# A hybrid encoder step on one core: queues filled in the order of the kernel's own estimate, with measured durations

## The chip, the cores and the metric

The kernel runs on one core of a Trainium2 chip. The metric is the device time of one execution in microseconds (us). Engines: TensorE (PE) multiplies matrices, VectorE (DVE), ScalarE (ACT) and GpSimd (POOL) work on elements, SyncE (SP) issues most transfers. Each engine runs its own queue of instructions in the order in which the program was written out; an instruction waits for semaphores of the others.

## The reference

One inference step of a two-layer encoder for 512 prompt tokens and 32 sample tokens, model width 1024, all in float32:

```python
def run_trunk(x, pos, mem_k, mem_v, states, ln_g, ln_b, ffn_up, ffn_down, xa_q, xa_o, mixer_params):
    for layer in range(DEPTH):
        x = post_norm(x, 0.5 * swiglu(x, ffn_up[layer, 0], ffn_down[layer, 0]), ln_g[layer, 0], ln_b[layer, 0])
        if layer % 2 == 0:
            y, st = mixer_ab(x, pos, *states[layer], *mixer_params[layer])
        else:
            y, st = mixer_c(x, *states[layer], *mixer_params[layer])
        x = post_norm(x, y, ln_g[layer, 1], ln_b[layer, 1])
        x = post_norm(x, cross_attn(x, mem_k[layer], mem_v[layer], xa_q[layer], xa_o[layer]), ...)
        x = post_norm(x, 0.5 * swiglu(x, ffn_up[layer, 1], ffn_down[layer, 1]), ln_g[layer, 3], ln_b[layer, 3])
```

`post_norm` is a layer norm of `ALPHA * x + sub`, `swiglu` has 2816 inner features, `cross_attn` 4 heads over 256 memory rows. `mixer_ab` is a gated linear recurrence (RG-LRU) beside a chunkwise retention. `mixer_c` is RWKV-7: projections and low-rank gates, and then for each token and each of 16 heads of 64

```python
def step(S, inp):
    r_t, w_t, k_t, v_t, kk_t, b_t = inp
    sa = jnp.einsum('bhvk,bhk->bhv', S, -kk_t)
    S = S * w_t[:, :, None, :] + sa[..., None] * b_t[:, :, None, :] + v_t[..., None] * k_t[:, :, None, :]
    return S, jnp.einsum('bhvk,bhk->bhv', S, r_t)
```

Outputs are the trunk's results for both token sets, the memory's keys and values of both layers, and all the states.

## The kernel before

**Tiling.** Tokens are columns, features are partitions. Half A holds 256 prompt tokens, half B the other 256 and the 32 sample tokens (288 columns). Weights come in granules of 128 output features and 1024 input features. ScalarE writes a granule's rounded copy, VectorE or GpSimd the remainder (`_split`), and a linear layer takes 24 PE products per granule and half: three products of the parts times eight blocks of the input. Stages in order: ffn00, mix0, xa0, ffn10 for layer 0, ffn01, mix1, xa1, ffn11 for layer 1. The halves run staggered, so that the products of one half stand under the norms, the attention and the recurrences of the other. PSUM tiles are named mm (linear layers and the recurrence's preparation) and ax (the rest); names in the listings end in numbers that only tell buffers apart. XA, XHA and XLA are half A's values and their split parts, XB and so on half B's; within the recurrence these names stand for the space that it takes over.

**What sets the order.** Each piece of work is a Python generator, a task. Its operations go through methods such as `mm`, `tt`, `gtt`, `act`: each calls `plan` with an engine and a duration. `Clock.op` puts the operation into the first gap on the engine's line of time after its operands are ready, and the start it finds becomes the instruction's priority; tasks of a negative band see a line on which only they stand. The task that is earliest by this clock runs next. `ett` asks the clock which of VectorE and GpSimd would be through first and takes that engine, so a duration can also choose an engine. After everything is emitted, the tile framework fills each engine's queue: line 2082 asks it to do so by a simulation of its own (`schedule_with_timeline_sim=True`), which takes the priorities as a ranking among what it finds ready.

**The recurrence.** It runs in chunks of 32 tokens, in blocks of 64: four blocks of A, four of B, and one of the 32 sample tokens; nine blocks, 17 chunks. Per block, `wkv_prep` (line 1797) works out keys and decays, starting with a GpSimd multiplication (arena from HLA or HLB and pv, 128x512), and makes 16 products per quarter (64x64) that give a triangular matrix; it is stored to scratch memory (dn). `wkv_solve` (line 1873) loads it (P from dn), inverts it by 31 pairs of dependent GpSimd steps on P and LC, stores the result (dz from LC) and loads it as transposed blocks (W from dz). `wkv_load` transposes keys and values, `wkv_chain` (line 1947) carries the state through the chunks, its first product on the solved block being ax from arena and W (128x64); `wkv_norm` does the head norm. Half B's low-rank gates are 128x288 products of XB and HHB with HLB and VB.

Of the kernel before, what the change touches and what calls it, by code (L numbers as in the profile page):

```python
# [102 lines left out]
class Res:  # L103
    """Things that are taken and given back, with the times from which they are free."""
# [27 lines left out]
class Line:  # L132
    """The spans of time in which an engine is taken; a later comer may fill a gap."""
# [28 lines left out]
class Clock:  # L162
    """An estimate of when instructions run, in ns: what an engine does and what its operands wait for.
    It orders the emission and the engines' queues, and nothing else rests on it."""
# [24 lines left out]
    def ready(self, outs, ins=()):  # L189
        """When the operands of a transfer are free and written."""  # L190
        t = self.now
        for ap in ins:
            c, q, f = self.area(ap)
            t = max(t, c[0, q, f].max())
        for ap in outs:
            c, q, f = self.area(ap)
            t = max(t, c[:, q, f].max())
        return t

    def renew(self, old, new):  # L200
        """A tile takes over the room of an older one."""
# [47 lines left out]
class Arena:  # L249
# [26 lines left out]
    def top(self, n):  # L276
        """The last n elements."""
# [50 lines left out]
class Arenas:  # L328
    """Several arenas as one."""
# [44 lines left out]
class Kern(Clock):  # L374
# [13 lines left out]
    def mm(self, out, lhsT, rhs, start=True, stop=True):  # L388
        n = free_size(rhs)
        if lhsT.dtype == F32R:  # L390
            cost = (n if n >= 256 else max(4 * n, 128)) / 2.4 + 2
        else:
            cost = 4 * (max(n, 62) / 2.4) + 2
# [8 lines left out]
    def _v(self, out, ins, fast=False):  # L402
        fast = fast and all(t.space != PSUM for t in ins)
        self.plan("v", 70 + free_size(out) / (1.92 if fast else 0.96), [out], ins)
# [5 lines left out]
    def gtt(self, out, a, b, op=ALU.mult):  # L410
        self.plan("g", 150 + free_size(out) * 2.0, [out], [a, b])
        self.nc.gpsimd.tensor_tensor(out, a, b, op=op)  # L412

    def ett(self, out, a, b, op=ALU.mult, lag=0.0):
        """On the engine that is through first; GpSimd has to be ahead by some ns."""
# [5 lines left out]
        dv, dg = 70 + n / 0.96, 150 + n * 2.0  # L421
# [27 lines left out]
    def gmemset(self, out, v):  # L449
        self.plan("g", 50 + free_size(out) * 0.83, [out], [])  # L450
        self.nc.gpsimd.memset(out, v)

    def scan(self, out, a, b, ini):
        self._v(out, [a, b])
# [16 lines left out]
    def act(self, out, a, f=AF.Copy, bias=None, scale=1.0, accum=None):  # L471
        dur = (60 if a.space == PSUM else 100) + free_size(out) / 1.2
        dur += 93 * ((bias is not None and not isinstance(bias, float)) + (not isinstance(scale, float)))
# [25 lines left out]
    def sigmoid(self, out, a, bias=None, half=None):  # L499
        """1 / (1 + exp(-a - bias)) = (1 + tanh((a + bias) / 2)) / 2; half: bias / 2."""  # L500
# [66 lines left out]
    def lend(self, slots, raws):  # L567
        """Slots and buffers of the weights for another use."""
# [9 lines left out]
    def stream(self, granules, after=(), limit=None, first=0):  # L578
        """Granules that are loaded one after another, from when the streams before them are through."""
# [5 lines left out]
    def pump(self):  # L585
        """Loads of weights and their splits, as far ahead as the room allows; when the next one can go."""
# [16 lines left out]
    def _load(self, s):  # L603
        """Loads a granule, or says when it could."""
# [46 lines left out]
    def linear(self, hf, xh, xl, kc=8, m=128):  # L651
        """One granule of the main stream against a half's split columns: a PSUM bank."""
# [49 lines left out]
def load_params(K):  # L702
    """Vectors of features as columns of one tile, by way of rows of 128 and transposes."""
# [125 lines left out]
def streams(K, gran, at):  # L829
    """Granules are loaded once for both halves, but for stretches of SOLO where one half is ahead, so  # L830
    that its products fill the other one's waits: for norms, attention and the recurrences."""
# [54 lines left out]
def split(K, hi, lo, src, k=0):  # L886
    """src = hi + lo, each with the 12 bits that a float32r product takes."""
# [7 lines left out]
def load_x(K, h):  # L895
    """Rows of x by way of the room for the products, as columns and their split."""
# [52 lines left out]
def store_states(K):  # L949
    """The states that were collected as columns."""  # L950
# [51 lines left out]
def out_piece(K, h, j, ps, first=True, last=True):  # L1002
    """x <- ALPHA * x + sub, a part of sub at a time.

    With the last part go the sums for the norm: the columns are shifted by the mean c of their first half,
    so that the mean of squares less the squared mean cancels no more than a bit."""
# [46 lines left out]
def rsqrt2(K, out, v, tmp, eps=None):  # L1053
    """out = -2 / sqrt(v + eps): exp(-ln / 2) and a Newton step."""
# [67 lines left out]
def mem_kv(K):  # L1122
    """Keys and values of the memory, both layers: features first in scratch (keys), rows first out.

    It fills the others' gaps, so it keeps a weight slot, a load buffer and a PSUM bank of its own."""
# [64 lines left out]
def give_kv(K, *tags):  # L1190
    """Slots' space for the split keys of a head and for its split values."""
# [45 lines left out]
def attend(K, h, l, hd, q, hh, hl, c0, m, qe, fin):  # L1237
    """Columns c0..c0+m of a half against one head's memory: prompt's own or the sample's cache.
    The weights of the values take the queries' place."""
    nc = K.nc  # L1240
# [83 lines left out]
def setup_mix0(K):  # L1324
# [26 lines left out]
    # -8 softplus(-lam) = -8 (max(-lam, 0) + 2 atanh(u / (2 + u))), u = exp(-|lam|)  # L1351
# [148 lines left out]
def rsqrt_small(K, out, v, tmp, eps):  # L1500
    """1 / sqrt(v + eps) for few columns: a guess from the bits and three Newton steps."""
# [100 lines left out]
def lora_weights(K, h):  # L1602
    """The first factors of the low-rank gates, as they are and with the mix of tokens folded in."""
# [91 lines left out]
def wkv_norm(K, w):  # L1695
    """The heads' norm, the bonus and the gate, 64 tokens at a time."""
# [34 lines left out]
def wkv(K):  # L1731
    """RWKV-7's recurrence by chunks of 32 tokens, 64 tokens prepared at a time.
# [355 lines left out]
```

## Time and profile before

| what | us |
|---|---|
| median of three runs | 3022.41 (3020.9 to 3025.26) |
| span of the profiled execution | 3028.7 |
| PE busy | 2833.4 |
| VectorE busy | 1743.4 |
| ScalarE busy | 1276.8 |
| GpSimd busy | 830.1 |

The page divides the span into 40 slices of about 76 us. PE is at 9 tenths nearly everywhere; the slices in which it is lower lie at 500 to 800 us (layer 0's mixer and attention) and at 1860 to 2540 us (the recurrence of layer 1). The clock granted to PE, too, is below full in these places alone. PE work that runs at half clock counts as busy for twice as long, so busy time and clock are read together.

### The profile page before, as it was taken

Reading aid. Unit: us, or ns where it says so; the run is one execution under the profiler, and the core shown is the slowest. Engines: PE = TensorE matmul, PEld = TensorE weight load, DVE = VectorE, ACT = ScalarE, POOL = GpSimd, SP = SyncE. Lnnn points to the kernel's source line nnn. Section 1 sums busy time; section 2 is a strip of 40 time slices with the busy share of each in tenths; the row PEclk is TensorE's granted clock in tenths of the full one; section 3 lists DMA queues with packets and bytes.
Section 4 is the critical chain, followed back from the end, with each engine's and each line's share of the span. In section 5 each row is a group of like instructions: output and inputs, shape, how many; then the busy total and the mean of one; then the engine's idle time right before and its main releaser. Section 6 shows DMA issues by size and latency. Waiting matters only on the chain.

```text
span 3028.7 us, 54637 instructions
## 1 busy us (share of the span) xinstructions
PE 2833.4 (94%) x22456; PEld 2716.3 (90%) x22456; DVE 1743.4 (58%) x3099; ACT 1276.8 (42%) x2184; POOL 830.1 (27%) x1088
## 2 busy tenths in 40 slices
PE   9999998998999999999999898888878889999998
PEld 8999998998998999989999897776767779998997
DVE  5333337677767333365355756674675666767655
ACT  4223233665545222234244343343435455655544
POOL 2001104333313000032011212466375543422301
PEclk9999999999999999999999998788778879999999
DMA  6443443322332232322356453122223135645563
GB/s 182 126 119 115 130 119 97 88 68 81 98 98 84 85 90 84 89 87 77 90 155 179 120 168 106 39 65 62 69 73 87 49 98 174 177 141 157 169 176 93
DMA packets 626331, 330.56 MB, mean 109 GB/s; under 512 B 45480, under 2 KB 620160, under 8 KB 626080
## 3 DMA queue, kind: packets, MB, share of 16 engines
q1 hardware_dynamic: 617952, 317.06, 36.8%
q0 software_dynamic: 3488, 9.44, 1.0%
q8 instruction: 176, 2.88, 0.4%
q10 hardware_dynamic: 4640, 0.56, 0.1%
q14 instruction: 75, 0.61, 0.1%
HBM read 313.09 MB, written 13.92 MB: 108 GB/s over the span
## 4 chain that ended last, share of the span: by engine, by line
PE 66%; DVE 10%; POOL 9%; DMA 7%; ACT 5%; issue 3%; SPq 0%; ACTq 0%; DVEq 0%; POOLq 0%
PE mm L395 60%; PE ax L395 4%; POOL LC L412 3%; POOL P L412 3%; DMA P<-dn 3%; DVE W L408 2%; ACT arena L486 1%; ACT W L486 1%; DVE arena L408 1%; DMA wr<-in_ffn_up 1%; PE ax L400 1%; DVE arena L432 1%; POOL arena L412 1%; ACT L2049 1%; DVE XB L408 1%
## 5 line engine op out<-in xcount | busy, mean ns | idle before, releaser
L486 ACT ACTIVATE W<-wr 128x1024 fp32r<-128x1024 f32 (+1 forms) x558 | 577.0, 1038 | 737.4 <-PE mm L395 560.0
L408 DVE TENSOR_TENSOR W<-wr,W 128x1024 fp32r<-128x1024 f32 (+1 forms) x455 | 561.5, 1236 | 551.7 <-ACT W L486 542.8
L395 PE MATMUL mm<-XHB,W 128*128 128x288 f32 x3840 | 585.1, 302 | 14.1 <-ACT XHB L486 4.7
L395 PE MATMUL mm<-XHA,W 128*128 128x256 f32 x3840 | 538.4, 290 | 28.9 <-ACT XHA L486 11.6
L395 PEld LDWEIGHTS mm<-XHB,W 128*128 128x128 f32 x3840 | 532.4, 191 | 25.0 <-ACT XHB L486 5.8
L395 PEld LDWEIGHTS mm<-XHA,W 128*128 128x128 f32 x3840 | 499.7, 194 | 39.7 <-ACT XHA L486 16.0
L412 POOL TENSOR_TENSOR W<-wr,W 128x1024 fp32r<-128x1024 f32 (+1 forms) x103 | 251.0, 2439 | 606.2 <-ACT W L486 550.6
L395 PE MATMUL mm<-XLB,W 128*128 128x288 f32 x1984 | 318.7, 300 | 0.7 <-DVE XLB L408 0.7
L395 PE MATMUL mm<-HHB,W 128*128 128x288 f32 x1920 | 291.0, 301 | 11.4 <-ACT W L486 4.4
L395 PEld LDWEIGHTS mm<-XLB,W 128*128 128x128 f32 x1984 | 283.0, 190 | 3.2 <-DVE XLB L408 1.1
L395 PE MATMUL mm<-XLA,W 128*128 128x256 f32 x1984 | 284.7, 283 | 0.0
L395 PEld LDWEIGHTS mm<-HHB,W 128*128 128x128 f32 x1920 | 267.0, 191 | 15.0 <-ACT W L486 5.3
L395 PE MATMUL mm<-HHA,W 128*128 128x256 f32 x1920 | 265.7, 288 | 5.9 <-POOL W L412 2.2
L395 PEld LDWEIGHTS mm<-XLA,W 128*128 128x128 f32 x1984 | 259.1, 190 | 0.3 <-DVE XLA L408 0.2
L395 PEld LDWEIGHTS mm<-HHA,W 128*128 128x128 f32 x1920 | 247.1, 192 | 8.8 <-POOL W L412 2.6
L486 ACT ACTIVATE arena<-mm 128x256 f32<-128x256 f32 (+4 forms) x292 | 112.2, 387 | 305.1 <-PE mm L395 287.5
L432 DVE SCALAR_TENSOR_TENSOR arena<-mm,arena 128x288 f32<-128x288 f32 (+1 forms) x176 | 77.2, 439 | 157.7 <-PE mm L395 149.0
L395 PE MATMUL mm<-HLB,W 128*128 128x288 f32 x896 | 144.3, 301 | 0.3 <-DVE HLB L408 0.3
L412 POOL TENSOR_TENSOR P<-LC,P 128x66 f32<-128x66 f32 (+24 forms) x279 | 113.5, 407 | 84.6 <-DMA P<-dn 64.6
L395 PEld LDWEIGHTS mm<-HLB,W 128*128 128x128 f32 x896 | 130.1, 193 | 0.6 <-DVE HLB L408 0.5
L395 PE MATMUL mm<-HLA,W 128*128 128x256 f32 x896 | 129.3, 284 | 0.0
L412 POOL TENSOR_TENSOR LC<-LC,P 128x66 f32<-128x66 f32 (+24 forms) x279 | 115.0, 412 | 20.5
(426 smaller groups left out, 3612.0 us busy)
## 6 DMA issues: line engine op xcount, KB each, us to landing
wr<-in_ffn_up SPq DMA_DIRECT2D x246, 512.0 KB
wr<-in_ffn_down SPq DMA_DIRECT2D x96, 448.0 KB
wr<-in_l_w_rkv SPq DMA_DIRECT2D x48, 512.0 KB
wr<-in_ffn_down SPq DMA_DIRECT2D x40, 512.0 KB
wr<-in_l_w_in SPq DMA_DIRECT2D x24, 512.0 KB
wr<-in_l_w_out SPq DMA_DIRECT2D x24, 512.0 KB
wr<-in_xa_q SPq DMA_DIRECT2D x24, 512.0 KB
wr<-in_xa_o SPq DMA_DIRECT2D x24, 512.0 KB
```

Of the source, the lines that this page charges most:

```text
L395: self.nc.tensor.matmul(out, lhsT, rhs, start=start, stop=stop)
L400: self.nc.tensor.transpose(out, in_, self.ident[k0:k0 + k, k0:k0 + k])
L408: self.nc.vector.tensor_tensor(out, a, b, op=op)
L412: self.nc.gpsimd.tensor_tensor(out, a, b, op=op)
L432: self.nc.vector.scalar_tensor_tensor(out, a, s, b, op0=op0, op1=op1)
L486: return self.nc.scalar.activation(out, a, f, bias=bias, scale=scale, **kw)
L2049: nc.scalar.preload_act_table_set(name)
```

## The change

Two edits. The durations that the methods hand to `plan` are replaced by others: a float32r product of 256 columns and more costs n/2.4 + 13 ns instead of n/2.4 + 2, a small float32 product at least 108 ns divided by `side`, the number of products that the array takes side by side; VectorE's fixed part is 147 ns instead of 70, GpSimd's 190 + 2.1 n instead of 150 + 2 n, ScalarE's 165 or 204 instead of 60 or 100, and a scan has a cost of its own. And the framework's own simulation is switched off, so that the queues are filled by the priorities. Docstrings and comments are dropped, which moves line numbers below `mm` by one. No operation is added or removed but that a few splits of weights change engines.

```diff
-    def mm(self, out, lhsT, rhs, start=True, stop=True):
+    def mm(self, out, lhsT, rhs, start=True, stop=True, side=1):
+
         n = free_size(rhs)
         if lhsT.dtype == F32R:
-            cost = (n if n >= 256 else max(4 * n, 128)) / 2.4 + 2
+            cost = n / 2.4 + 13 if n >= 256 else max(4 * n / 2.4, 108.0) + 2
         else:
-            cost = 4 * (max(n, 62) / 2.4) + 2
+            cost = max(4 * n / 2.4, 108.0) / side + 2
...
-        self.plan("v", 70 + free_size(out) / (1.92 if fast else 0.96), [out], ins)
+        self.plan("v", 147 + free_size(out) / (1.92 if fast else 0.96), [out], ins)
...
-        self.plan("g", 150 + free_size(out) * 2.0, [out], [a, b])
+        self.plan("g", 190 + free_size(out) * 2.1, [out], [a, b])
...
-        dv, dg = 70 + n / 0.96, 150 + n * 2.0
+        dv, dg = 147 + n / 0.96, 190 + n * 2.1
...
-        self.plan("g", 50 + free_size(out) * 0.83, [out], [])
+        self.plan("g", 95 + free_size(out) * 0.86, [out], [])
...
-        self._v(out, [a, b])
+        self.plan("v", 195 + free_size(out) * 2.0, [out], [a, b])
...
-        dur = (60 if a.space == PSUM else 100) + free_size(out) / 1.2
-        dur += 93 * ((bias is not None and not isinstance(bias, float)) + (not isinstance(scale, float)))
+        dur = (165 if a.space == PSUM else 204) + free_size(out) / 1.2
+        dur += 88 * ((bias is not None and not isinstance(bias, float)) + (not isinstance(scale, float)))
...
-            K.mm(pr[32 * q:32 * q + 32, g * 64:g * 64 + 64], X[0:96, hd, 32:64], Y[0:96, hd])
+            K.mm(pr[32 * q:32 * q + 32, g * 64:g * 64 + 64], X[0:96, hd, 32:64], Y[0:96, hd], side=4)
...
-    with tile.TileContext(nc, schedule_with_timeline_sim=True) as tc:
+    with tile.TileContext(nc, schedule_with_timeline_sim=False) as tc:
```

How the order moves, at two places. The first is PE's queue at the first solve: from the last key products of block 0 (XLA, 64x64) to the first product on the solved block (ax from arena and W, 128x64). Before, some rows of the stretch, its end whole:

```order
L395 MATMUL mm_64<-XLA_17671 64x64 x8
L395 MATMUL mm_66<-XLA_17671 64x64 x8
...
L395 MATMUL ax_70<-XB_98,HLB_17823 128x288
L395 MATMUL ax_70<-HHB_17886,HLB_17823 128x288
L400 MATMUL ax_67<-identt,VA_16458 32x128 x4
...
L395 MATMUL mm_65<-XHB_99,W_3_73 128x288 x8
L395 MATMUL mm_65<-XLB_100,W_3_73 128x288 x8
...
L395 MATMUL mm_63<-XLB_100,W_4_74 128x288 x8
L395 MATMUL mm_65<-XHB_99,W_3_73 128x288
L395 MATMUL ax_68<-arena_79,W_114_17676 128x64 x4
L395 MATMUL mm_64<-W_111_17673 64x64 x8
```

The change's queue at the same place:

```order
L396 MATMUL mm_64<-XLA_17549 64x64 x7
L401 MATMUL ax_70<-identt,XLA_17549 128x64 x8
L396 MATMUL mm_65<-HHB_13222,W_4_74 128x288 x5
...
L396 MATMUL ax_69<-XB_98,HLB_17946 128x288
L396 MATMUL mm_63<-W_110_17550 64x64
L396 MATMUL mm_64<-W_110_17550 64x64
L396 MATMUL ax_67<-arena_79,W_114_17554 128x64 x3
L401 MATMUL ax_70<-identt,W_110_17550 128x64 x4
...
L396 MATMUL ax_69<-HHB_18159,HLB_17946 128x288
L396 MATMUL ax_69<-XB_98,HLB_17946 128x288
```

Before, 32 of half B's gate products and 49 products of its linear granules stand between the two; now one gate product and 12 granule products, and the other gate products stand behind the product on the solved block.

The second place is GpSimd's queue around a solve of half B: the 31 pairs of steps on P and LC, and the first multiplication of a later block's preparation (arena from HLB and pv). Before, inside the sixth solve:

```order
L412 TENSOR_TENSOR LC_7380<-LC_7380,P_115_17677 128x7x6
L412 TENSOR_TENSOR P_115_17677<-LC_7380,P_115_17677 128x35
L412 TENSOR_TENSOR arena_79<-HLB_19016,pv 128x512
L412 TENSOR_TENSOR LC_7380<-LC_7380,P_115_17677 128x7x5
L412 TENSOR_TENSOR P_115_17677<-LC_7380,P_115_17677 128x28
```

The change, ahead of the seventh solve's first step:

```order
L452 MEMSET LC_7380 128x256
L452 MEMSET LC_7380 32x8 x4
L413 TENSOR_TENSOR W_1_71<-wr_76,W_1_71 128x1024
L413 TENSOR_TENSOR arena_79<-HLB_19268,pv 128x512
L413 TENSOR_TENSOR P_115_17555<-LC_7380,P_115_17555 128x31
L413 TENSOR_TENSOR LC_7380<-LC_7380,P_115_17555 128x31
```

The multiplication moved out of the dependent steps, to a place ahead of the first of them.

More of the change, by code (lines that the diff above doesn't have):

```diff
@@ L1993, in wkv_chain @@
             g, q = divmod(k, 2)
-            K.mm(b1[64 * q:64 * q + 64, g * 64:g * 64 + 64], KL[64:128, 8 * q + g], Y[64:128, 8 * q + g])
+            K.mm(b1[64 * q:64 * q + 64, g * 64:g * 64 + 64], KL[64:128, 8 * q + g], Y[64:128, 8 * q + g], side=2)
         pc = PC.rearrange("p j e -> p (j e)")
@@ L2002, in wkv_chain @@
             j, e = divmod(hd, 2)
-            K.mm(pr[64 * e:64 * e + 64, j * 32:j * 32 + 32], Y[:, hd], X[:, hd, 0:32])
+            K.mm(pr[64 * e:64 * e + 64, j * 32:j * 32 + 32], Y[:, hd], X[:, hd, 0:32], side=2)
         K.act(h.k[:, :, t0 + 32 * c:t0 + 32 * c + 32], pr.rearrange("p (j t) -> p j t", j=8))
```

## The prediction

> **What bounds the kernel now.** I read the page's engine totals and slices first, then the windows by stage, then the chain of waits, then the timelines of TensorE (PE), GpSimd (POOL) and the DMA queues inside the slow stage. The profiled execution has a span of 3028.7 us; the median of the three runs is 3022.41 us, 6.3 below it. I work out differences on the profiled execution and add them to the median.
>
> ```profile
> span 3028.7 us, 54637 instructions
> PE 2833.4 (94%) x22456; PEld 2716.3 (90%) x22456; DVE 1743.4 (58%) x3099; ACT 1276.8 (42%) x2184; POOL 830.1 (27%) x1088
> ...
> 480.00:1000.00 520.00, 482.94 (x3636) 467.81 (x3636) 367.52 (x923) 277.78 (x559) 176.10 (x175) 0.96 0.29 86
> 1000.00:1340.00 340.00, 340.00 (x2691) 339.84 (x2690) 127.09 (x188) 90.68 (x141) 14.60 (x16) 1.00 0.30 87
> ...
> 1860.00:2200.00 340.00, 284.89 (x2322) 238.90 (x2321) 233.59 (x418) 139.28 (x250) 180.40 (x338) 0.80 0.24 59
> 2200.00:2540.00 340.00, 288.54 (x2687) 252.69 (x2685) 218.87 (x396) 159.15 (x291) 179.32 (x354) 0.83 0.33 91
> ```
>
> A windows row gives the stretch, its length, the busy time of PE, PEld, DVE, ACT and POOL, then the granted clock of PE and the DMA share. The dense stage 1000 to 1340 has PE busy for all its 340 us at clock 1.00: no order of the queues can make it shorter or longer unless it breaks it. The recurrence of the second layer, 1860 to 2540, is the other kind: PE busy 573.4 of 680 us, at a granted clock of 0.80 and 0.83. At full rate its work would take about 284.89 x 0.80 + 288.54 x 0.83 = 467 us, so about 210 us go there. This is where an order can win or lose.
>
> The loop there is one solve per 64 tokens, nine in all. The first one, from the last key product of block 0 to the first product on its solved block:
>
> ```profile
> 1894.49 3.67 PE L395 MATMUL mm<-XLA 64*64 64x64 f32 x32
> ...
> 1898.92 0.33 SPq L491 DMA_DIRECT2D dn<-XLA  x1
> 1900.68 0.63 SPq L491 DMA_DIRECT2D P<-dn  x1
> ...
> 1900.68 9.14 DMA P<-dn
> ...
> 1909.89 0.84 POOL L412 TENSOR_TENSOR P<-LC,P 128x31 f32<-128x31 f32 x1 [6.49 <-DMA P<-dn]
> ...
> 1940.01 0.21 POOL L412 TENSOR_TENSOR LC<-LC,P 128x8 f32<-128x8 f32 x1
> 1940.17 1.04 POOL L412 TENSOR_TENSOR arena<-HLA,pv 128x512 f32<-128x512 f32 x1
> 1940.24 0.54 SPq L491 DMA_DIRECT2D dz<-LC  x1
> 1944.94 0.81 SPq L491 DMA_DIRECT2D W<-dz  x2
> ...
> 1949.59 1.80 PE L395 MATMUL ax<-arena,W 128*128 128x64 f32 x8
> ```
>
> The keys are done at 1898.2 (1894.49 + 3.67), go through memory and back by 1909.89, the 62 dependent GpSimd steps last until 1940.22 (30.3 us), the solved block goes out and back, and PE uses it at 1949.59. That is a latency of **51.4 us**, nearly uninterrupted, whatever PE does meanwhile. PE's queue runs in order, so what matters is how much work stands in that queue between the two ends.
>
> **The change, part by part.** *The machine and the durations* act only through the order; the products are the same 20844. In the order, steps by which PE's rows go back against the kernel's own estimate fall from 489 to 305, and the mean displacement from that estimate falls from 16.3 to 4.0 places (with the old durations and the new filling 3.7, with the new durations and the old filling 12.4). So the new filling does nearly what it says, and the durations are the smaller edit.
>
> *What stands under the first solve.* From the listing shown above: the 31 gate products of half B (128x288 f32) and 37 of 49 products of B's linear granules stood there before and stand behind it now. Their price is the spacing of these rows:
>
> ```profile
> 1914.31 0.65 PE L395 MATMUL ax<-XB,HLB 128*128 128x288 f32 x2
> 1914.80 0.65 PE L395 MATMUL ax<-HHB,HLB 128*128 128x288 f32 x2
> ...
> 1931.52 1.22 PE L395 MATMUL mm<-XLB,W 128*128 128x288 f32 x8
> 1932.58 0.83 PE L395 MATMUL mm<-XHB,W 128*128 128x288 f32 x5
> ```
>
> 0.485 us and 1.06/8 = 0.133 us each: 15.0 + 4.9 = 19.9 us, with some small products 24. In all, 32.5 us of full-rate work stood in that window, now 8.5. I did the same sum over the nine windows of the listing. Before: 32.5, 43.4, 46.4, 44.6, 39.2, 37.6, 47.3, 40.3, 53.6 (385 us). After: 8.5, 38.9, 45.6, 39.7, 14.7, 28.3, 30.0, 31.0, 51.3 (288). The other 97 us now lie between the windows or behind them, because the next block's key products stand *behind* the product that waits for the solve; the work between such a product and the next block's last key product was 24 us in all and is 112: 13.2 among A's four blocks, 63.4 from A's last to B's first (31.9 before), 35.7 among B's five. Solve and cover thus run more one after another. A strict order by estimate has no reason to put cover under a wait that the estimate takes to be shorter.
>
> *Their sum.* Read off as for the first window, whose ends stand above, the nine measured windows are 51.4, 60.8, 75.5, 63.4, 60.2, 71.7, 60.1, 56.8, 76.6: each at the floor of 51.4 or above, 113 above in all. The last ends at 2506.03. The windows rows of A's part, the turn and B's part, with the granted clock last but two:
>
> ```profile
> 2506.03 1.00 PE L395 MATMUL ax<-arena,W 128*128 128x64 f32 x8
> ...
> 1898.20:2132.70 234.50, 200.32 (x1684) 165.93 (x1684) 147.60 (x269) 97.19 (x176) 139.31 (x288) 0.83 0.25 59
> 2132.70:2172.00 39.30, 36.17 (x375) 31.06 (x374) 29.12 (x42) 17.82 (x32) 12.29 (x7) 0.89 0.30 83
> 2172.00:2506.00 334.00, 278.91 (x2471) 240.71 (x2472) 218.14 (x412) 151.33 (x282) 189.12 (x379) 0.79 0.28 75
> ```
>
> With each window at its floor and the work between them at these clocks: A's four, 4 x 51.4 + 13.2/0.83 = 221.5, for 234.5 now (-13.0). The turn to B, 63.4/0.89 + the 3.5 us that 39.3 now exceeds 31.9/0.89 by = 74.7 (+35.4). B's five, 5 x 51.4 + 35.7/0.79 = 302.2, for 334.0 (-31.8). Behind the last window 8.5 us more work is left. Sum: **-0.9 us**. So the floors gained pay for the cover lost, and the sign lies in what the windows still take above 51.4.
>
> *What speaks for a gain: the stalls at a queue's head.*
>
> ```profile
> 1941.24 0.63 ACT L486 ACTIVATE arena<-arena 128x512 f32<-128x512 f32 x1 [15.68 <-POOL arena L412]
> 1942.22 0.41 PE L400 MATMUL ax<-identt,ov 128*48 128x128 f32 x1 [7.85 <-ACT TGB L486]
> ...
> 2009.40 0.64 PE L395 MATMUL ax<-Q,W 96*32 96x64 f32 x10 [6.97 <-ACT HLA L486]
> ...
> 2271.92 0.63 ACT L486 ACTIVATE arena<-arena 128x512 f32<-128x512 f32 x1 [17.62 <-POOL arena L412]
> 2274.14 2.08 PE L395 MATMUL ax<-HLB,centt 128*128 128x512 f32 x2 [9.88 <-ACT HLB L486]
> ...
> 2476.88 1.44 PE L395 MATMUL mm<-XHA,W 128*128 128x256 f32 x5 [7.26 <-POOL W L412]
> ```
>
> A prep's first multiplication (arena from HLA or HLB, 1.04 us) sits in the middle of a solve on POOL, ACT's square waits for it at the head of its queue for 15.68 or 17.62 us, and PE waits behind ACT. In the new order this multiplication stands ahead of a solve's first step, never inside one. About 33 foreign POOL steps stood inside solve loops (7 of them splits of weights), now about 13 (1 split). The nine loops:
>
> ```profile
> L412 POOL TENSOR_TENSOR P<-LC,P 128x66 f32<-128x66 f32 (+24 forms) x279 | 113.5, 407 | 84.6 <-DMA P<-dn 64.6
> L412 POOL TENSOR_TENSOR LC<-LC,P 128x66 f32<-128x66 f32 (+24 forms) x279 | 115.0, 412 | 20.5
> ```
>
> They are busy for 228.5 us, and from first to last step they take 316, where nine of 30.3 would be 273: 43 of the 113 us above the floors are there. At 13/33 of it 17 us stay, some 13 of them in windows other than the third and the last. In those two PE's own work decides: 45.6/0.83 = 54.9 and 51.3/0.89 = 57.6, 3.5 and 6 us above the floor. Together I take **+23 us** above the floors for the nine windows, between 0 (no stall left) and 113 (all stay).
>
> *The norms.* Between the last product of a half's sub-layer and the next one that needs its norm, the other half has to cover some 17 us, as here, from the end of A's products (1338.68 + 1.00) to the first of the next sub-layer:
>
> ```profile
> 1338.68 1.00 PE L395 MATMUL mm<-HLA,W 128*128 128x256 f32 x7
> ...
> 1356.81 1.44 PE L395 MATMUL mm<-XHA,W 128*128 128x256 f32 x6
> ```
>
> In the listing this cover falls in most places, B's first from 18.4 to 9.4 us, A's first from 9.3 to 7.4, B's fifth from 10.1 to 4.0. Cover that is missing costs time only where nothing else stands ready in PE's queue, so I take about a third of it, +5 us; bounds: 0, and 17 (9.0 + 1.9 + 6.1, all of it).
>
> *Elsewhere.* The window 480 to 1000 leaves 37 us of PE idle and 19 at the missing clock, 56 in all. Truer durations may give some back or lose some; I take 0, bounds -17 and +17, a third of it.
>
> *Engines and tables.*
>
> ```profile
> L412 POOL TENSOR_TENSOR W<-wr,W 128x1024 fp32r<-128x1024 f32 (+1 forms) x103 | 251.0, 2439 | 606.2 <-ACT W L486 550.6
> L408 DVE TENSOR_TENSOR W<-wr,W 128x1024 fp32r<-128x1024 f32 (+1 forms) x455 | 561.5, 1236 | 551.7 <-ACT W L486 542.8
> L2049 ACT ACT_TABLE_LOAD x56 | 71.8, 1283 | 1.0
> ```
>
> Five splits go from POOL to VectorE: -12.2 us there, +6.2 on an engine busy 58%, covered by PE's work. ScalarE loads 6 tables more, 6 x 1.28 = 7.7 us on an engine busy 42%; they lie under PE's work where it has cover, and in a norm's chain without cover they would cost up to these 7.7. I take 0.
>
> The sum: -0.9 + 23 + 5 = **+27 us**, 3022.4 + 27 = about **3050 us**, slower by 0.9%.
>
> *The clock.* The windows rows show a clock of 1.00 where PE never waits and 0.80 to 0.83 where gaps of 7 to 10 us stand. The Trainium skill, "TensorE: Matmul & The Clock Gate", Part 1 (The HAM clock gate), says that the array falls to half rate after about 3.4 us of idling and comes back after about as much activity. The trace agrees with the first half. That rule speaks against the change: under the first and fifth solve PE's idle time grows, and at an estimate from that page each return would cost up to 1.7 us, some 15 us over nine windows. My sum goes without it, by the measured clocks.
>
> **The rivals.**
>
> *Faster, about 2990 us.* Nothing is left above the floors, and PE's work between the windows runs at full rate: A 205.6 + 13.2 = 218.8 (-15.7), the turn 66.9 (+27.6), B 257 + 35.7 = 292.7 (-41.3), 8.5 behind: -20.9. With +5 for norms and -17 elsewhere: -33 us. For it: the quoted stalls all start at a POOL step that the new order moves. Against it: the clock of 0.79 to 0.89 belongs to the serial pattern, and that grows.
>
> *No change, about 3022 us.* The windows keep only some 5 us above their floors and the norms lose nothing, or the listing's order matters little since a scheduler still fills the queues and still steps back 305 times.
>
> *Slower by far, about 3127 us.* Excess in eight windows stays at 12.6 us (113/9) because it is not POOL's order but the waits before the load of the keys and after the solved block: -0.9 + 101 + 5 = +105. It decides from 1 us per window on: each us above the floor costs 9. For it: 70 of the 113 us lie outside the loops. Against it: part of these 70 is PE's work itself, which shrinks by 97 us.
>
> **How the numbers follow.** The forecast of 3050 gets 0.38, faster 0.37, no change 0.13, slower by far 0.12. About 0.2%, 6 us, is what a measurement of this kernel can tell from no change. So: faster 0.37, same 0.13, slower 0.50. The forecast's own range is 3010 (no excess, elsewhere -17) to 3095 (excess of 70: -0.9 + 70 + 5). Since cases of both signs hold most of the chance, the whole range reaches from 2972, below the faster case by its -17 once more, to that 3095.
>
> **What would show it.** In the changed profile: right, if the first window of the recurrence shows PE idle for about 40 us with the solve's latency still at 51 us, the turn from A to B takes 70 us or more, and the ACT waits of 11 to 18 us behind a multiplication on POOL are gone. Excess: the nine windows should lie between 51 and 60 us. Wrong, if the windows come out below 50, if PE in 1860 to 2540 is busier than 573 us, if the recurrence (607.8 us from block 0's keys to the last solved block) becomes shorter by more than 10 us, or if the difference lies outside it, above all in 480 to 1000.

## The result and the profile after

The changed kernel takes 3241.41 us (median of four runs, 3232.19 to 3246.62), the kernel before 3023.2 us: a ratio of 1.072, 95% interval 1.0699 to 1.0741. It is slower by 218 us. The page of the changed kernel, and its windows at the places shown of before (columns as there; line numbers are one higher):

```profile
span 3244.9 us, 54624 instructions
PE 2940.9 (91%) x22456; PEld 2783.8 (86%) x22456; DVE 1760.2 (54%) x3097; ACT 1290.7 (40%) x2190; POOL 788.6 (24%) x1090
...
PE   8999998898999999999998984797877679999998
...
PEclk9999999999999999999999976687767769999999
```

```profile
480.00:1000.00 520.00, 474.31 (x3541) 454.74 (x3540) 373.61 (x913) 276.76 (x553) 173.31 (x179) 0.97 0.28 84
1000.00:1340.00 340.00, 340.00 (x2695) 339.87 (x2694) 119.01 (x177) 88.78 (x139) 10.94 (x11) 1.00 0.30 87
1860.00:2200.00 340.00, 260.39 (x1955) 209.58 (x1953) 182.46 (x318) 109.87 (x194) 134.29 (x296) 0.73 0.18 46
2200.00:2540.00 340.00, 273.12 (x1950) 228.77 (x1951) 190.06 (x337) 122.55 (x228) 128.72 (x228) 0.72 0.22 61
```

The dense stage is what it was, PE busy 340 of 340 us. The recurrence is thinner: PE busy less, its clock 0.73 and 0.72 for 0.80 and 0.83, and it now reaches on to 2701. The span is 216.2 us longer. 41.4 of these are there when the first block's last key product ends (1939.6, before 1898.2), 153.9 come between that and the first product on the last solved block (761.7 us, before 607.8), and 20.9 behind it.

```profile
1939.60:1992.80 53.20, 13.12 (x75) 8.94 (x75) 28.02 (x56) 13.57 (x23) 30.24 (x72) 0.56 0.21 46
1939.60:2220.60 281.00, 203.61 (x1570) 161.08 (x1571) 144.38 (x259) 89.64 (x161) 120.50 (x290) 0.71 0.18 46
2220.60:2318.00 97.40, 89.60 (x669) 77.21 (x668) 57.82 (x95) 37.68 (x68) 25.66 (x17) 0.81 0.28 83
2318.00:2701.30 383.30, 291.79 (x2198) 239.96 (x2198) 199.74 (x377) 135.94 (x257) 171.41 (x370) 0.70 0.21 57
```

These are the first solve's window, A's part, the turn to B, and B's part: 281.0, 97.4 and 383.3 us for 234.5, 39.3 and 334.0 before.

For the rest I use one table that I worked out from the traces of all PE products: the time from each product's start to the next one's, less the first one's time at full rate (the spacing of like products in a row at a granted clock of 1.00, as in the prediction). What is left is loss. It is split into gaps of 2 us and more, and into smaller losses: where a granule's product (float32r) stands next to another kind (small float32 products, transposes), between granule products, and between the others. In brackets the count. With somewhat other prices for the small products the differences between kernels move by some 10 us a column, so they are estimates.

| kernel | gaps of 2 us and more | change of kind | granule to granule | other to other | all |
|---|---|---|---|---|---|
| before | 130.5 (30) | 41.6 (571) | 102.3 | 81.5 | 355.9 |
| the change | 217.6 (35) | 129.8 (899) | 148.6 | 75.0 | 571.0 |
| filling only (e1) | 220.8 (34) | 121.3 (897) | 140.8 | 58.9 | 541.9 |
| durations only (e2) | 170.0 (38) | 38.7 (613) | 116.4 | 53.6 | 378.7 |
| bursts (e4) | 234.1 (33) | 68.4 (601) | 126.6 | 65.4 | 494.5 |
| bursts, transfers, SP (e10) | 213.3 (42) | 57.1 (542) | 124.1 | 52.5 | 447.0 |

So the loss has two parts of one size, longer waits (+87 us) and more and dearer changes of kind (+88 us), and a smaller third, +46 us between granule products, most of it where the granted clock is low. The low clock is in the other columns too; the table does not take it out of them.

**The changes of kind.** PE's timeline within A's third solve, changed kernel:

```profile
2098.49 0.69 PE L396 MATMUL mm<-SUMA,LC 64*128 64x64 f32 x4
2099.11 0.61 PE L396 MATMUL mm<-XHB,W 128*128 128x288 f32 x1
2099.65 0.69 PE L396 MATMUL mm<-SUMA,LC 64*128 64x64 f32 x2
2100.26 0.61 PE L396 MATMUL mm<-XHB,W 128*128 128x288 f32 x1
2100.80 0.69 PE L396 MATMUL mm<-SUMA,LC 64*128 64x64 f32 x2
2101.42 0.61 PE L396 MATMUL mm<-XHB,W 128*128 128x288 f32 x1
...
2124.34 2.12 PE L396 MATMUL mm<-XLB,W 128*128 128x288 f32 x8
2126.39 1.11 PE L401 MATMUL ax<-identt,XHA 64*128 64x64 f32 x8
```

The same products in the kernel before:

```profile
1906.35 3.61 PE L395 MATMUL mm<-SUMA,LC 64*128 64x64 f32 x32
```

Sixteen of these small products (two records each) took 3.61 us in one burst, 0.23 each, at a granted clock of 1.00. (At 0.50 a burst of them takes 3.68 us in run e4 below: there its products start two at a time, 7 ns apart, which they didn't in the kernel before.) Put one by one between granule products, a pair of one small and one granule product takes 1.15 us (2099.65 to 2100.80) at 0.50. A granule product in a row of eight takes 0.26 us a little later (2124.34 to 2126.39), so the two in rows of their own kind would be 0.49 us. A small product that stands alone cannot start beside another; how much of the difference that is was not measured. The whole order listing of the change shows such alternations, and I read from it only how much work stood at a place, not how it was mixed.

**The waits.** Some of ScalarE's waits, with total, count and longest in us; first the kernel before, then the changed one:

```profile
ACT arena L486 <- POOL arena L412: 96.8, 32, 17.6
ACT HLA L486 <- DMA dz<-LC: 11.0, 1, 11.0
ACT HHB L486 <- DMA dz<-LC: 5.9, 1, 5.9
ACT XHA L486 <- DMA dz<-LC: 4.7, 1, 4.7
```

```profile
ACT arena L487 <- POOL arena L413: 49.2, 35, 3.1
ACT arena L487 <- DMA dz<-LC: 45.1, 2, 23.2
ACT HLB L487 <- DMA dz<-LC: 21.2, 1, 21.2
ACT XHA L487 <- DMA dz<-LC: 15.2, 1, 15.2
ACT wr L487 <- DMA dz<-LC: 13.7, 1, 13.7
```

The stalls behind a multiplication on GpSimd are gone as forecast (longest 3.1 for 17.6 us). Another head of the same queue took their place: ScalarE issues two of the four loads of each solved block (W from dz, `adma`). They wait for the block's store, and what stands behind them waits too: 95 us, 22 before. Under the first two solves this stops PE:

```profile
1990.01 0.63 ACT L487 ACTIVATE arena<-arena 128x512 f32<-128x512 f32 x1 [21.87 <-DMA dz<-LC]
...
2050.27 0.38 ACT L487 ACTIVATE arena<-ax 128x256 f32<-128x256 f32 x1 [23.24 <-DMA dz<-LC]
```

```profile
1992.14 0.69 PE L396 MATMUL mm<-W 64*64 64x64 f32 x4 [32.61 <-DVE W L409]
...
2050.70 1.97 PE L396 MATMUL ax<-arena,W 128*128 128x64 f32 x8 [17.64 <-ACT arena L487]
```

At 1992 it is the next block's preparation that ScalarE holds up, by way of VectorE; at 2050 it is the chain's own copy for the block that was already solved, which waited for loads of the next one.

### The profile page after: what moved, and what is told of

It is laid out like the page before. It is cut to its first block, busy times and chain, and to the rows that moved or that the text cites. A ratio compares the mean times of both kernels' runs of the same rounds, so it can differ in the third digit from the quotient of the medians.

```text
span 3244.9 us, 54624 instructions
## 1 busy us (share of the span) xinstructions
PE 2940.9 (91%) x22456; PEld 2783.8 (86%) x22456; DVE 1760.2 (54%) x3097; ACT 1290.7 (40%) x2190; POOL 788.6 (24%) x1090
## 4 chain that ended last, share of the span: by engine, by line
PE 54%; DVE 9%; POOL 8%; DMA 5%; issue 3%; ACT 2%; ACTq 0%; SPq 0%; POOLq 0%; DVEq 0%
PE mm L396 48%; PE ax L396 5%; POOL LC L413 3%; POOL P L413 3%; DMA P<-dn 2%; PE ax L401 2%; DVE W L409 1%; DVE XA L409 1%; DVE arena L433 1%; DVE arena L409 1%; ACT arena L487 1%; DMA dz<-LC 1%; ACT W L487 1%; DVE XB L409 1%; DVE P L409 0%
## 5 line engine op out<-in xcount | busy, mean ns | idle before, releaser
L396 PE MATMUL mm<-XHB,W 128*128 128x288 f32 x3840 | 601.8, 307 | 21.9 <-ACT W L487 17.4
L396 PE MATMUL mm<-XHA,W 128*128 128x256 f32 x3840 | 554.7, 294 | 52.0 <-ACT XHA L487 38.1
L396 PEld LDWEIGHTS mm<-XHB,W 128*128 128x128 f32 x3840 | 544.2, 195 | 32.7 <-ACT W L487 18.7
L396 PEld LDWEIGHTS mm<-XHA,W 128*128 128x128 f32 x3840 | 507.4, 196 | 67.4 <-ACT XHA L487 42.0
L413 POOL TENSOR_TENSOR W<-wr,W 128x1024 fp32r<-128x1024 f32 (+1 forms) x98 | 234.6, 2395 | 919.9 <-ACT W L487 830.5
L396 PE MATMUL mm<-XLA,W 128*128 128x256 f32 x1984 | 298.0, 290 | 6.8 <-POOL XLA L413 4.8
L396 PE MATMUL mm<-HHA,W 128*128 128x256 f32 x1920 | 276.4, 293 | 6.2 <-DVE W L409 3.2
L487 ACT ACTIVATE arena<-mm 128x256 f32<-128x256 f32 (+3 forms) x292 | 112.8, 388 | 346.2 <-PE mm L396 321.6
L396 PEld LDWEIGHTS mm<-HLB,W 128*128 128x128 f32 x896 | 129.8, 192 | 3.1 <-issue 1.0
L413 POOL TENSOR_TENSOR P<-LC,P 128x66 f32<-128x66 f32 (+24 forms) x279 | 102.1, 366 | 105.1 <-DMA P<-dn 84.4
L409 DVE TENSOR_TENSOR arena<-arena 128x256 f32<-128x256 f32 (+3 forms) x137 | 97.7, 714 | 53.3 <-ACT arena L487 51.5
```

Of the source, the lines that this page charges most:

```text
L396: self.nc.tensor.matmul(out, lhsT, rhs, start=start, stop=stop)
L409: self.nc.vector.tensor_tensor(out, a, b, op=op)
L487: return self.nc.scalar.activation(out, a, f, bias=bias, scale=scale, **kw)
```

## The experiments

Filling and durations first, each alone.

```diff
# e1: the kernel before, only
-    with tile.TileContext(nc, schedule_with_timeline_sim=True) as tc:
+    with tile.TileContext(nc, schedule_with_timeline_sim=False) as tc:
# e2: the changed kernel, only
-    with tile.TileContext(nc, schedule_with_timeline_sim=False) as tc:
+    with tile.TileContext(nc, schedule_with_timeline_sim=True) as tc:
```

> The kernel before with one edit: the queues are filled strictly by the kernel's own estimate; its old durations stay. Theory A (the strict filling is the cause): about as slow as the whole change, 3200 to 3280 us; full-rate work in PE's queue under the nine solves is 272 us in this order, as in the change (288), against 385 before. Theory B (the new durations are the cause, since they mislead the estimate): 3020 to 3060 us.

> The changed kernel with one edit taken back: the framework's simulation fills the queues again, ranked by the new estimate. Theory A: within 40 us of before, 2990 to 3060 us, as 374 us of work stand under the solves (385 before). Theory B: 3150 us and more.

Measured: e1 3217.13 us, 1.0653 of before (1.0626 to 1.0681); e2 3054.31 us, 1.0110 (1.0095 to 1.0125). Theory A holds: the filling costs some 196 us, the durations 33, and both together 218. In e1 the table's losses are those of the change; in e2 the changes of kind cost no more than before.

Then the estimate of a solve, which takes its three transfers for some 10 us less than the trace shows:

```diff
-            e = lo.put(s + 1000.0, dur) + dur + 900.0
+            e = lo.put(s + 1000.0, dur) + dur + 900.0 + self.lag
```

`self.lag`, in ns, is set to 5500 around the load of the keys, to 2400 around the store of the solved block and to 2200 around its loads, and is 0 elsewhere.

> The changed kernel, whose estimate takes the transfers of each solve as long as the profile before shows them: 5.5 us more for the load of the keys, 2.4 for the store of the solved block, 2.2 for its loads; no instruction differs but in its place. Theory A1 (the strict order loses because the estimate takes a solve for some 10 us too short, nine times, so that waiting products stand too early): about 3241 - 9 x 10 = 3150 us, with the sum of the windows from a block's keys to its solved block, 584 us in the changed kernel, falling below 530. Theory A2 (strict order loses whatever the solve's estimate, since any late operand stops a whole queue): 3220 to 3260 us.

Measured: 3210.37 us, 1.0623 (1.0605 to 1.0641), 31 us below the change. The windows from a block's keys to its solved block did not shrink (601 us in sum, 584 in the change); what shrank is the work between them. The total lies in neither theory's range: A1 explains about a seventh of the loss, and A2's range began 10 us higher. Most of the loss was still without a reason, and a rule was needed for what stops the queue. The alternation in the trace gave one:

```diff
+        if eng == "pe":
+            end = s + dur
+            if self.burst is not None and self.burst[0] == self.turn and s - self.burst[2] < 250.0:
+                s = self.burst[1]
+            self.burst = (self.turn, s, end)
+        else:
+            self.burst = None
         self.tc.cur_priority = 10000000 + int(s) + ...
```

> The changed kernel, where TensorE products that one task emits back to back (gaps below 0.25 us in the estimate) all get the priority of the first of them, so that single products of another task are not put between them. Changes between a granule product (float32r) and another kind fall from 918 to 616 in PE's queue, in the last 1000 us from 643 to 351; the work under the solves stays 290 us (288). Theory S (each such change costs PE some 0.2 us with the lower clock that goes with it): 3140 to 3180 us. Theory L (only late operands at the queue's head cost): 3225 to 3255 us.

> The same bursts in the kernel whose estimate takes the solve's transfers as measured (3210 us). Changes of kind 532, work under the solves 323 us. Theory S: 3100 to 3140 us. Theory L: 3180 to 3210 us, for the 13 us of work more under the solves.

> The kernel before with the same bursts: its old durations and the framework's simulation. Changes of kind fall only from 588 to 546, since the simulation keeps bursts together by itself; work under the solves 381 us (385). Theory S: 3005 to 3025 us. Theory L: the same as before within 10 us.

Measured: e4 3170.41 us, 1.0485 (1.0464 to 1.0506); e5 3154.26 us, 1.0429 (1.0407 to 1.0451); e6 3047.65 us, 1.0078 (1.0060 to 1.0096). The edit of e4 touches only the priorities of PE's products; the other queues moved a little with them (some 180 of ScalarE's 2208 entries and 190 of VectorE's 3097 stand in another order). 71 us came back; the changes of kind cost 68.4 us for 129.8, the sixteen small products run in one burst again, and the clock over the recurrence rises from 0.72 to 0.76. The row of the burst, then the windows row of the recurrence, in e4, and that row in the change and in the kernel before:

```profile
2080.22 3.68 PE L404 MATMUL mm<-SUMA,LC 64*128 64x64 f32 x32
...
1923.00:2636.60 713.60, 513.22 (x4455) 435.35 (x4455) 403.96 (x733) 268.62 (x489) 325.89 (x677) 0.76 0.22 60
```

```profile
1939.60:2701.30 761.70, 585.00 (x4433) 478.25 (x4433) 401.94 (x729) 263.26 (x484) 317.57 (x677) 0.72 0.21 56
```

```profile
1898.20:2506.00 607.80, 515.41 (x4528) 437.70 (x4528) 394.85 (x722) 266.35 (x489) 340.72 (x674) 0.81 0.27 69
```

PE is busy for 72 us less than in the change with nearly the same products, and no longer than before (513 and 515 us). But PE's idle time in the recurrence is 200 us, 177 in the change and 92 before. So bursts took back what the mixing cost PE, and left the waits as long as they were, or longer. Theory S's range is met for the changed filling, and in the table 61 of the 77 us that came back are changes of kind; theory L's range is not. e5 lies between its two theories' ranges, 14 us above that of S: transfers and bursts together give 87 us, not the 102 of both alone. e6 missed on the other side: the simulation kept bursts together by itself, so there was little to win, and the step from the sixth solved block to the seventh took 30 us more (92 for 62 us).

Next, an order without any filling:

```diff
-    with tile.TileContext(nc, schedule_with_timeline_sim=False) as tc:
+    with tile.TileContext(nc, schedule_with_timeline_sim=False, linearize=True) as tc:
```

> The changed kernel, whose queues are the order in which its tasks emit their operations, without any filling by the framework: a task's operations stay together, and tasks go in the order of the estimate. Changes of kind fall from 918 to 354, steps back against the estimate on PE from 307 to 132, work under the solves rises from 288 to 327 us. Theory S: 3060 to 3130 us. Theory L (a fixed order loses to late operands, more so if it follows the estimate more strictly): 3200 us and more.

Measured: 11155.33 us. PE is busy 39% of the span, VectorE, ScalarE and GpSimd 15, 12 and 6%, so in this form the engines run nearly one after another, which is more than each queue in the order of emission. It tells nothing on S or L; whether a truly strict order by the estimate would do better stays untried.

Then the head of ScalarE's queue:

```diff
-            (K.dma, K.adma)[q % 2](w.tb[b % 2][32 * q:32 * q + 32, :4 * nch, 32 * q:32 * q + 32], dq[q, :, :4 * nch])
+            K.dma(w.tb[b % 2][32 * q:32 * q + 32, :4 * nch, 32 * q:32 * q + 32], dq[q, :, :4 * nch])
```

> The changed kernel, where all four loads of a solved block are issued by SyncE, not two of them by ScalarE. In the changed kernel's trace ScalarE stands idle for 95 us with such a load at its queue's head (releaser: the store of the solved block; 22 us in the kernel before), up to 23.2 us at a time, and once TensorE waits 17.6 us behind it. Theory H (these waits hold up the recurrence's own copies): 3185 to 3215 us. Rival (the wait only moves to SyncE, where the weights' loads stand behind it, or the recurrence has to wait for the solve anyway): 3230 to 3260 us.

> Bursts kept together, the solve's transfers estimated as measured (3154 us), and all four loads issued by SyncE. There ScalarE waited 162 us with such a load at its head. Theory H: 3095 to 3130 us. Rival: 3140 to 3165 us.

> The kernel before with all four loads issued by SyncE. Its ScalarE waits only 22 us with such a load at its head, in three places. Theory H: 3005 to 3018 us. Rival: 3020 to 3040 us.

Measured: e9 3231.71 us, 1.0686 (1.0666 to 1.0706); e10 3123.13 us, 1.0333 (1.0316 to 1.0350); e11 3029.88 us, 1.0024 (1.0014 to 1.0035). ScalarE's waits for dz are gone in all three. Alone this gives 10 us, within the rival's range, where theory H asked for 26 at least; on top of bursts and transfers it gives 31, within H's range. The trace bears the rival out too: in e9 the last key product of the eighth block is done at 2527.9, but the store of these keys is issued at 2543.9, behind SyncE's own loads from dz and of weights; in e10 the sixth block loses 18 us so (2268.5 to 2286.8). Over the nine blocks this step takes 44 us in e9 and 22 in the change, while the step from the last load to the product falls from 114 to 84. In e10 the recurrence takes 654 us, for 761.7 in the change and 607.8 before:

```profile
1922.80:2576.80 654.00, 487.76 (x4384) 413.65 (x4384) 397.38 (x738) 260.08 (x481) 314.79 (x665) 0.77 0.24 62
```

PE stands idle for 166 us of these 654. In the table the changes of kind are nearly back where they were before (57.1 for 41.6 us), the gaps are not (213.3 for 130.5): ScalarE's queue is free, and most of the waiting is still there. That SyncE's loads give 31 us here and 10 alone I read so: while changes of kind hold PE up as well, a copy that comes earlier meets a PE that is not ready for it. That reading is argued, not shown, since work under the solves rose too, from 323 to 348 us. In e11 there was little waiting to remove, and it lost 6 us.

More cover under the solves:

> The last but one with the solve's transfers estimated at twice the added time (11.0, 4.8 and 4.4 us), so that more work is put under the solves: 431 us at full rate, against 348 in that kernel, 288 in the changed one and 385 in the one before. Theory C (what is left of the loss is cover that stands behind the solved block's first product): 40 to 80 us faster than that kernel, near 3060 us. Rival (the windows only grow with their content, as PE works at the lower clock there): within 20 us of that kernel or slower.

Measured: 3168.28 us, 1.0474 (1.0457 to 1.0491), 45 us slower than e10. The windows grew to 726 us in sum (615 in e10). Theory C falls: what is left of the loss is not cover in the wrong place, or not to be had by an estimate of the solve that is too long.

The clock behind an idle stretch:

```diff
+                if b == 1 and c == 0 and q == 0:
+                    K.tc.cur_priority = 10000000 + int(K.now)
+                    for _ in range(64):
+                        nc.tensor.matmul(ps[:, 0:256], K.ident, K.g2[:, 0:256], start=True, stop=True)
```

> The changed kernel with 64 products more (128x256 f32, at full rate some 27 us), whose result is overwritten, in TensorE's queue under the first solve, where TensorE stood idle for 32.6 us. They compute nothing of the reference. Theory K (after an idle stretch the lower clock stays for some 20 us, as from 1992 to 2012 in the changed kernel, so each idle stretch costs some 10 us behind it): the rows behind the first solved block run at clock 1.00 within 3 us, and the kernel is 5 to 15 us faster than the changed one in spite of the added work. Rival (the lower clock comes from the small products themselves): clock 0.50 there as before, total 3235 to 3260 us. The queue's order behind the place shifts too, by which the total can move either way; the clock at the place decides.

Measured: 3246.43 us, 1.0744 (1.0719 to 1.0770), the same as the change. The windows of the place:

```profile
1955.00:1965.00 10.00, 2.02 (x4) 1.14 (x5) 6.41 (x16) 2.31 (x5) 7.13 (x21) 0.50 0.08 22
1965.00:1970.00 5.00, 5.00 (x16) 3.97 (x15) 4.96 (x9) 2.73 (x5) 4.63 (x5) 0.59 0.00 0
1970.00:1975.00 5.00, 5.00 (x25) 4.41 (x24) 1.77 (x3) 0.00 (x0) 4.18 (x11) 1.00 0.00 0
1975.00:1995.00 20.00, 20.00 (x100) 17.39 (x99) 4.65 (x16) 1.26 (x2) 8.11 (x33) 1.00 0.09 14
```

The products on W behind the filler, and the same in the changed kernel:

```profile
1994.46 2.08 PE L396 MATMUL mm<-W 64*64 64x64 f32 x32
```

```profile
1994.84 3.24 PE L396 MATMUL mm<-W 64*64 64x64 f32 x28
```

With full-size products the clock is back within some 5 us and stays at 1.00 as the solved block arrives; 32 records of W take 2.08 us there, where 28 of them took 3.24 in the change. At the place, theory K holds against its rival. The 5 to 15 us that it promised in total did not come: the order moved behind it, and a wait of 10.1 us followed at 2007.87.

Last, what the kernel before bears:

```diff
# e14: the kernel before, with the lag of e3
# e15: the kernel before, with only TensorE's new durations (three calls get a `side` of 2 or 4)
-            cost = (n if n >= 256 else max(4 * n, 128)) / 2.4 + 2
+            cost = n / 2.4 + 13 if n >= 256 else max(4 * n / 2.4, 108.0) + 2
...
-            cost = 4 * (max(n, 62) / 2.4) + 2
+            cost = max(4 * n / 2.4, 108.0) / side + 2
```

> The kernel before, whose estimate takes the solve's transfers as measured, with its old durations and the framework's simulation. Theory A1 there too (the estimate of the solve is too short): 3000 to 3015 us. Rival (the simulation has its own view of transfers, the estimate is but a ranking): 3015 to 3045 us.

> The kernel before with TensorE's new durations alone, the framework's simulation stays. The new durations together cost 33 us. Theory P (TensorE's part does it, since it makes a packed product a quarter or half of a small one): 3040 to 3070 us. Rival (the element engines' part does it): 3015 to 3030 us.

Measured: e14 3052.95 us, 1.0104 (1.0082 to 1.0127); e15 3065.66 us, 1.0138 (1.0121 to 1.0154). Truer transfers cost 29 us here. TensorE's durations alone cost 42 us, more than all new durations together (33), so theory P names the part, but the parts do not add up. Under the old filling each of the five edits to the estimate or a queue (e2, e6, e11, e14, e15) lost 6 to 42 us, those with truer numbers as well.

No run beat the kernel before.

## Why the prediction was right and wrong

The sign was right, the size was not: +27 us was forecast and 216 came in the profiled execution, far outside the range. The sign was in part luck: without the +23 us that turned out mis-sized, the prediction's sum was +4, and it gave slower no more than 0.50. By the prediction's steps, in us, forecast and measured:

| step | forecast | measured |
|---|---|---|
| ahead of the recurrence (the norms, 480 to 1000) | +5 | +41.4 |
| nine windows, in sum | 485.6 (floors 462.6 and 23) | 584.3 |
| work between them | 135.8 | 177.4 |
| of this the turn from A to B | 74.7 | 97.4 |
| behind the last window | +8.5 | +20.9 |

- **The first solve** went as said: latency 53.2 us, PE busy for 13.1 of them, so idle for 40.
- **The serial work** was read right from the order, 112 us of full-rate work between the windows, for 24 before. (Both are net: where the next block's keys are done ahead of the product on the solved block, the stretch counts as negative.) It was priced with the clock of before, 0.83, 0.89 and 0.79; the parts ran at 0.71, 0.81 and 0.70. At these clocks the same sum gives 151 us for 136, and 177 were measured: the other 26 us had no term in the sum.
- **The step that failed most** is "+23 us above the floors": it was 122, the 113 of before once more. The part that I worked out, the foreign steps on GpSimd inside the solve loops, did better than forecast: the nine loops took 260 us, where I said 290 and before had 316. But of the 70 us of excess outside the loops the prediction kept only 9.5 us, in two windows, and gave no better reason than that PE's work there shrinks. They became 134: from the last key product to the first step the nine windows take 146 us, 135 before; from store to last load 64, 48 before; from the last issued load of a solved block to the product on it 114, 78 before. ScalarE's blocked queue is one cause of this (in A's third block its load came 17.5 us behind the store), work in front of the waiting product is another; how much each has, no run divides, as e9 frees the queue but moves part of the wait to SyncE. "Slower by far" had this reason and the excess right (12.6 us per window forecast there, 13.5 measured) and ended at 3127 us, for want of the steps that follow. How the loss falls to the windows and to the work between them is itself a matter of the order: in e1 the windows sum to 518 us, only 56 above the floors, and the work between them to 210, and e1 is nearly as slow as the change.
- **What was not in the sum at all** is the mixture of kinds, +88 us in the table. These lie inside the rows above, in the windows and between them. It was visible blind: rows of a single product each, alternating, stood in the whole listing (918 changes of kind in PE's queue, 588 before).
- **The clock** stood only beside the sum, with 15 us by the Trainium skill's rule. The table's granule products alone lost 46 us more, most of it at the low clock. The Trainium skill, "TensorE: Matmul & The Clock Gate", Part 1 (The HAM clock gate), lets the full rate return after some 3.4 us of activity. The filler's trace comes near that (within 5 us, with 128x256 products); the changed kernel's does not, with 19 us of PE work at 0.50 after the gap that ends at 2050.70, shown below.
- **The norms.** Missing cover did show, and more than a third of it: 41.4 us is more than the upper bounds for norms and elsewhere together, 17 and 17. By equal numbers of granule products done, 12 of them are there by layer 0's mixer, 10 more by the norm at 1340, and the rest comes between 1500 and 1940. Which edit of the order does it was not tried; e1 has 55 us at this point and e2 saves 7, so it is the filling.
- **That a scheduler still fills the queues** was part of the rival of no change. It is partly so: the order of the changed kernel has PE's product on the first solved block, which the estimate starts at 1971.0, ahead of products that it starts at 1957.9.

What stays open: the 99 us by which e10 is still slower, of which 25 are there as the first keys are done, and with them the waits: PE is idle for 166 us of the recurrence there and was for 92 before, and no run took these waits back to that or names all of their causes. Open is also how the low clock divides between idle stretches and mixed products.

## What to carry to other kernels

An order is not only how much work stands under a wait. Read in the listing also which kinds stand side by side and what stands at the head of each queue, transfers that an engine issues above all. Truer numbers for a planner need not make a better order: under the old filling all five edits lost here. I guess that this order had been tuned around its planner's errors; no run tuned it again around the truer numbers. So try planner and numbers each alone before both.

## What the runs showed of the hardware

PE's clock fell while PE was busy without a gap (by the profile, which models where a product ends). The changed kernel's windows over the alternation above:

```profile
2080.00:2090.00 10.00, 10.00 (x116) 8.17 (x115) 7.98 (x10) 5.22 (x10) 4.36 (x3) 1.00 0.49 139
2090.00:2100.00 10.00, 9.76 (x62) 6.55 (x61) 5.32 (x7) 1.53 (x3) 8.67 (x19) 0.71 0.10 23
2100.00:2110.00 10.00, 10.00 (x32) 7.31 (x32) 2.03 (x6) 0.63 (x1) 8.04 (x26) 0.50 0.01 2
2110.00:2120.00 10.00, 10.00 (x69) 7.48 (x68) 3.57 (x5) 6.53 (x13) 6.41 (x21) 0.50 0.02 3
```

The longest gap there is 0.24 us, and yet the clock goes from 1.00 to 0.50 and stays there for some 37 us; for most of them single granule products and small float32 products take turns. After an idle stretch it is the same: busy, and low.

```profile
2050.00:2060.00 10.00, 9.29 (x54) 6.50 (x56) 3.83 (x7) 5.39 (x10) 1.57 (x4) 0.50 0.09 15
2060.00:2070.00 10.00, 10.00 (x117) 8.38 (x114) 4.42 (x7) 2.13 (x5) 0.00 (x0) 0.50 0.04 7
2070.00:2080.00 10.00, 10.00 (x58) 6.55 (x57) 3.89 (x7) 3.73 (x7) 0.00 (x0) 0.98 0.05 9
```

So being busy does not by itself keep the clock or bring it back: e13's full-size products brought it back in 5 us, the mixed work behind 2050.70 took 19. Nor does taking turns always lower it. Between these two stretches single granule products take turns with 64x64 products at 1.00:

```profile
2074.00:2077.00 3.00, 3.00 (x18) 1.90 (x17) 1.23 (x3) 1.09 (x2) 0.00 (x0) 1.00 0.04 8
...
2074.45 0.40 PE L396 MATMUL mm<-XLB,W 128*128 128x288 f32 x1
2074.78 0.33 PE L396 MATMUL mm<-XHA 64*64 64x64 f32 x2
```

What in the work decides is not shown by these runs. A change of kind also costs time at full clock: from the row at 2093.36 to that at 2094.05 one small and one granule product took 0.69 us, where the burst's 0.23 in the kernel before and the prediction's 0.133 make 0.36.

```profile
2093.00:2094.10 1.10, 1.10 (x8) 0.72 (x6) 0.62 (x2) 0.66 (x2) 0.94 (x4) 1.00 0.00 0
...
2093.36 0.43 PE L396 MATMUL mm<-SUMA,LC 64*128 64x64 f32 x2
2093.72 0.40 PE L396 MATMUL mm<-XHB,W 128*128 128x288 f32 x1
2094.05 0.51 PE L396 MATMUL mm<-SUMA,LC 64*128 64x64 f32 x2
```
